# Four heads' queries and decays as a fifth set of half products, turned by transposes, and all heads' by way of memory

## The chip, the cores and the metric

One core of one Trainium2 chip runs the kernel. The metric is device time in microseconds for one execution, as the median of several runs.

## What is computed

A decoder trunk of two layers on 512 positions of width 2048, all in float32. Layer 0 runs a convolution branch and an attention branch; the change doesn't touch it. Layer 1 is a gated linear recurrence (HGRN2) with 16 heads, state 128x128:

```
h = rmsnorm(x, od_norm_g)
q, f_raw, i_val, g = split(h @ od_w_in)        # 2048 x 8192: four parts of 2048 columns
logf = logaddexp(log(lb), log1p(-lb) + log_sigmoid(f_raw));  k = -expm1(logf)
# per head, with b = cumsum(logf):
#   A[t,s] = sum_k q[t,k] k[s,k] exp(b[t]-b[s])  for s <= t
#   o      = A @ v + (q*exp(b)) @ state
o = rmsnorm(o, norm_g) * silu(g)
x = x + o @ od_w_out
```

After it comes a final rmsnorm. In the kernel `oq` names the query columns, `of` those of the decay, `oi` the values, `og` the gates. Each head has 128 columns of each.

## The kernel before

Every product is made in three matmuls of a high and a low part (`mm3`: high x high, low x high, high x low), so that the float32r matmuls of TensorE (PE) keep float32 precision. Weights come in tiles of 128x1024: the high part is read as it is, the low part is formed by ScalarE (ACT, the negated high part) and a second read that adds in memory (`Loaded`), or by a subtraction on VectorE (DVE) (`Formed`).

Layer 1 has three stages. First `dense("oq", h, h1)` and `dense("of", h, h1)` make queries and decays of heads 0 and 1, features on partitions, and write them to a DRAM tile `qd`. A `dense` is 4 quarters, each of 4 blocks x 3 matmuls of 512 columns, and after each quarter `tick()` runs.

Then values and gates are made by `SETS`, four sets of half products: seven products of half-size blocks in place of eight (Strassen's way, with sums of activation blocks in `sums` and of weight blocks in `Formed`). A product has 4 weight tiles, each with 2 blocks x 2 banks x 3 matmuls of 512 columns. Here positions are on partitions. `result` adds, scales by the row's reciprocal deviation `r1`, applies the gate's function where it is a gate, and writes to the DRAM tiles `vd` and `gd`.

Last the heads. While `dense` makes queries and decays of heads 2 to 15 straight into SBUF tiles `q` and `kn` (`m` for odd heads), `hgrn` runs as a generator: each `tick()` advances every live chain by one `yield`, so that the chain's own matmuls stand in PE's row after a quarter's 12. `begin_chain` starts the next head when its decay exists (`begun`) and enough ticks have passed since the last start (`since`: 8 for the first five and the last four, 10 for the others). A chain has 14 pieces: decays and their running products within 4 (`pi`, `xe`), two reciprocals, scaled queries and keys (`qb`, `kb` in `rc`), key products (L1073), two levels of `radix4` (L1026), transposes of keys (L1090), state updates (L1096), outputs (L1106, L1108), norm, and transposes of the result (L1125) into `mix[h]`. `out_part` puts parts of the output projection `w_out("ow", ...)` between the projections by the table `SPREAD`; `w_out` ticks once per column block.

PE's instructions run in the order in which the program writes them. On the other engines and on the DMA queues a planner orders them by its own estimates of when each is ready; each engine and queue then runs in that fixed order. SyncE (SP) issues the reads and writes of `qd`, `vd`, `gd`, `vr`, `gate` and of the residual `xall`; GpSimd (POOL) issues those of most weights. PSUM has 5 banks for `mm` and 3 for `aux`, which the chains use.

Of the kernel before, what the change touches and what calls it, by code (L numbers as in the profile page):

```python
# [7 lines left out]
F32 = mybir.dt.float32  # L8
# [7 lines left out]
P = 128  # L16
# [9 lines left out]
RATE = 0.67  # L26
RATE0 = 0.4
MAN = "PE"
N_WTILES = 224
N_EARLY = 128  # L30
LAST = 2 * N_WTILES - NK
SETS = [("oi", 0), ("oi", 1), ("og", 0), ("og", 1)]


V_EVG, V_ODG, V_FING = 0, 16, 32
# [14 lines left out]
def trunk(ctx: ExitStack, tc: tile.TileContext, x, w, ws, vec, cst, rope, msk, out, order):  # L50
# [28 lines left out]
    def spawn(gen):  # L79
        chains.append(gen)  # L80
        return gen
# [178 lines left out]
            act.activation(t, src, AF.Square)  # L260
            eng.tensor_tensor(out=acc, in0=acc, in1=t, op=ALU.add)

    def rstd_chain(acc, n, r, dst, delay=0, scale=None):


        accs = acc if isinstance(acc, tuple) else (acc,)
        nb = accs[0].shape[-1] // P
        for _ in range(delay):
            yield
        ps = ps_x()  # L270
        for b in range(nb):
            for i, a in enumerate(accs):
                pe.matmul(ps[:, b:b + 1], a[:, blocks(b)], ones[:, 0:1], start=i == 0, stop=i == len(accs) - 1)
        m = sm.tile([P, 4], F32, name="rm", tag="rm")
        dve.tensor_scalar(m[:, :nb], ps[:, 0:nb], 1.0 / n, EPS, op0=ALU.mult, op1=ALU.add)
        pool.tensor_tensor(out=r[:, :nb], in0=m[:, :nb], in1=nhalf[:, :nb], op=ALU.pow)
        if scale is not None:
            dve.tensor_scalar(r, r, scale, None, op0=ALU.mult)
        yield
        ps = ps_x()  # L280
        dg = tmp("c")
        for b in range(nb):
            dve.tensor_scalar(dg[:, blocks(b)], ident, r[:, b:b + 1], None, op0=ALU.mult)
        yield
        for b in range(nb):
            pe.matmul(ps[:, blocks(b)], ones, dg[:, blocks(b)], start=True, stop=True)
        if dst is not None:
            act.activation(dst, ps[:, :nb * P], AF.Copy)
        return ps
# [543 lines left out]
    xtx = ExitStack()  # L833
    xt = xtx.enter_context(tc.tile_pool(name="xt", bufs=1, reuse_waits="tile"))
    tpc[:] = [xt, "c"]
    c1 = spawn(rstd_chain(acc1, D, r1, rb1, 2))
    sums = [(fp.tile([P, 3 * H], F32R, name=f"fh{k}", tag=f"fh{k}"), fp.tile([P, 3 * H], F32R, name=f"fl{k}", tag=f"fl{k}"))
            for k in range(8)]

# [21 lines left out]
            split_scaled(u[:, j, :H], vs[:, V_ODG + k:V_ODG + k + 1], h1[k][0][:, H:], h1[k][1][:, H:])  # L861


    qd = [dr.tile([P, 2, S], F32, name=f"qd{h}") for h in range(2)]
    for h in range(2):
        ps = dense("oq", h, h1)
        if h == 0:
            for k in range(4):
                x_sums(k)
            finish(c1)  # L870
        z = tmp("z")
        dve.tensor_tensor(out=z, in0=ps, in1=rb1, op=ALU.mult)
        nc.sync.dma_start(qd[h][:, 0, :], z)
        ps = dense("of", h, h1)
        if h == 0:
            for k in range(4, 8):
                x_sums(k)
            xctx.close()
            xtx.close()
            ph.append(sctx.enter_context(tc.tile_pool(name="ph", bufs=1, reuse_waits="tile")))  # L880
        nc.sync.dma_start(qd[h][:, 1, :], decay(h, ps, tp.tile([P, S], F32, name="gate", tag="gate", bufs=2)))
# [47 lines left out]
    def keep(tag, b):  # L929
        return ph[0].tile([P, S], F32, name=tag, tag=f"{tag}{b}")  # L930

    for s_ in range(4):
        p1, p2 = banks(), banks()
        for m in range(4):
            product(p1, "A11", m)
# [26 lines left out]
            result(s_, 1, b, p3[b], u[b])  # L962
        for b in range(2):
            result(s_, 1, 2 + b, p7[b], u[b])
        if s_ == 3:
            restore()
        p4 = banks()
        for m in range(4):
# [10 lines left out]
    def hgt(name, shape=(P, S), tag=None):  # L979
        return hg.tile(list(shape), F32, name=name, tag=tag or name)  # L980

    at = hgt("at", (P, 4, P))
    pool.memset(at, 0.0)

    def blk(t_, half):
        return t_.rearrange("p (n c) -> p n c", c=8)[:, :, half * 4:half * 4 + 4]

    def to_at(ps, groups, cols, m, b0, nb, o):

        n = P // (4 * m)  # L990
        ng = len(groups)
        w = nb * m
        src = ps[:, :ng * 192].rearrange("p (g a n c) -> p g a n c", g=ng, a=2, n=n)[:, :, cols[0], :, cols[1] * m:
                                                                                     cols[1] * m + w]
        dst = at[:, groups[0]:groups[-1] + 1, :].rearrange("p g (n c) -> p g n c", c=4 * m)[:, :, :, b0 * m:b0 * m + w]
        msk_ = mk[:, None, o:o + n * w].broadcast_to([P, ng, n * w]).rearrange("p g (n c) -> p g n c", c=w)
        dve.copy_predicated(dst, msk_, src)

    def radix4(X, ks, t, m, ab, o):


        n = S // (4 * m)
# [19 lines left out]
        for gg in ((0, 1), (2, 3)):  # L1022
            ps = ps_x()
            for i, g in enumerate(gg):
                rhs = X[:, :, blocks(g)].rearrange("p a (n c) -> p a n c", c=4 * m)[:, :, :, m:]
                pe.matmul(ps[:, i * 192:(i + 1) * 192], ks[:, blocks(g)], rhs, start=True, stop=True)  # L1026
            to_at(ps, gg, (0, 0), m, 1, 3, o)
            to_at(ps, gg, (1, 0), m, 2, 2, o + 96)
            to_at(ps, gg, (1, 2), m, 3, 1, o + 160)
# [4 lines left out]
    vrows = {}  # L1034

    def hgrn(h, kn, q, gate):
        f = hgt("f")
        dve.tensor_scalar(f, kn, -(1.0 - 2.0 ** -24), 1.0, op0=ALU.max, op1=ALU.add)

# [89 lines left out]
    heads = []  # L1129
    qk = {}  # L1130

    def qk_tiles(h):
        qk[h] = (hg.tile([P, S], F32, name="q", tag="q", bufs=2), tmp("m", bufs=1) if h % 2 else hgt("kn"))
        return qk[h]

    def start(h):
        gate = tp.tile([P, S], F32, name="gate", tag="gate", bufs=2)
        nc.sync.dma_start(gate.rearrange("p (b c) -> p b c", b=4), gd[h // 4][:, :, blocks(h % 4)])
        q, kn = qk[h]
        heads.append(spawn(hgrn(h, kn, q, gate)))  # L1140

    for h in range(2):
        for i, t in enumerate(qk_tiles(h)):
            nc.sync.dma_start(t, qd[h][:, i, :])


    SPREAD = {0: [(6, 1, 3), (7, 0, 3), (7, 1, 3), (8, 0, 3), (8, 1, 2), (9, 0, 2)],
              1: [(9, 1, 3), (10, 0, 3), (10, 1, 3), (11, 0, 3), (11, 1, 2), (12, 0, 2)]}
    begun = [2]
    since = [99]  # L1150

    def begin_chain():
        since[0] += 1
        n = len(heads)
        if n < begun[0] and since[0] >= (8 if n < 5 else 10 if n < 12 else 8):
            since[0] = 0
            start(n)

# [9 lines left out]
                    w_out("ow", list(range(4 * g, 4 * g + 4)), range(c, c + part[2]))  # L1168
                c += part[2]

    for h in range(2, 16):
        if h == 4:
            spawn(load_xa(xd))
        ps = dense("oq", h, h1)
        q, kn = qk_tiles(h)
        dve.tensor_tensor(out=q, in0=ps, in1=rb1, op=ALU.mult)
        out_part(h, 0)
        decay(h, dense("of", h, h1), kn)
        begun[0] = h + 1
        out_part(h, 1)  # L1180
    w_out("ow", [8, 9, 10, 11], range(NK))
# [87 lines left out]
def _weights(inp, order):  # L1269
# [61 lines left out]
```

## Time and profile before

| | before |
|---|---|
| median of 3 runs | 1765.04 us (1764.37 to 1766.46) |
| profiled execution, its own time | 1763.39 us |
| span, first to last instruction | 1761.6 us |
| mean granted TensorE clock | 0.994 |
| PE busy | 1731.8 us (98%) |
| DVE busy | 1208.7 us (69%) |
| ACT busy | 735.5 us (42%) |
| POOL busy | 224.2 us (13%) |

The span is what the profile divides into engines' busy and idle time; the execution's own time is 1.8 us longer. Matmuls overlap in the records: one of 512 columns shows some 390 ns, and the next starts 227 ns after it, so PE's pace is read from the starts.

### The profile page before, as it was taken

Reading aid. Unit: us, or ns where it says so; the run is one execution under the profiler, and the core shown is the slowest. Engines: PE = TensorE matmul, PEld = TensorE weight load, DVE = VectorE, ACT = ScalarE, POOL = GpSimd, SP = SyncE. Lnnn points to the kernel's source line nnn. Section 1 sums busy time; section 2 is a strip of 40 time slices with the busy share of each in tenths; the row PEclk is TensorE's granted clock in tenths of the full one; section 3 lists DMA queues with packets and bytes.
Section 4 is the critical chain, followed back from the end, with each engine's and each line's share of the span. In section 5 each row is a group of like instructions: output and inputs, shape, how many; then the busy total and the mean of one; then the engine's idle time right before and its main releaser. Section 6 shows DMA issues by size and latency. Waiting matters only on the chain.

```text
span 1761.6 us, 22265 instructions
## 1 busy us (share of the span) xinstructions
PE 1731.8 (98%) x8227; PEld 1436.4 (82%) x8227; DVE 1208.7 (69%) x2268; ACT 735.5 (42%) x1345; POOL 224.2 (13%) x290
## 2 busy tenths in 40 slices
PE   8999999999999999999999999999999999999997
PEld 6888888888888888887788888888888888888896
DVE  8554948594889895575777678877567555557666
ACT  6434444444343233375545455533332333323354
POOL 6000000000000000051000000022222222222200
PEclk9999999999999999999999999999999999999998
DMA  6222222222373323268777676796677787887642
GB/s 236 94 89 86 83 99 82 96 84 90 98 237 101 99 93 102 96 193 240 234 234 218 230 221 218 219 285 153 146 180 162 159 193 161 169 190 158 150 132 96
DMA packets 93932, 273.34 MB, mean 155 GB/s; under 512 B 9344, under 2 KB 22912, under 8 KB 92928
## 3 DMA queue, kind: packets, MB, share of 16 engines
q1 hardware_dynamic: 66176, 172.38, 29.1%
q0 software_dynamic: 27072, 98.58, 26.4%
q8 instruction: 64, 1.05, 0.2%
q10 hardware_dynamic: 576, 0.97, 0.2%
q14 instruction: 44, 0.36, 0.1%
HBM read 250.93 MB, written 20.97 MB: 154 GB/s over the span
## 4 chain that ended last, share of the span: by engine, by line
PE 86%; DVE 7%; DMA 3%; issue 2%; ACT 2%; POOL 1%; POOLq 0%; DVEq 0%; ACTq 0%
PE mm L225 24%; PE mm L227 24%; PE mm L226 24%; PE aux L226 2%; PE aux L225 2%; PE aux L227 2%; PE aux L1026 2%; DMA rw<-ws 1%; PE aux L458 1%; PE aux L1106 1%; DVE hl L249 1%; DVE wl L253 1%; PE aux L1096 1%; PE aux L1073 1%; DVE wq L253 1%
## 5 line engine op out<-in xcount | busy, mean ns | idle before, releaser
L252 ACT ACTIVATE wq<-raw 128x512 fp32r<-128x512 f32 x256 | 161.0, 631 | 349.9 <-PE mm L227 342.7
L253 DVE TENSOR_TENSOR wq<-raw,wq 128x512 fp32r<-128x512 f32 x256 | 183.9, 720 | 120.2 <-ACT wq L252 119.5
L225 PE MATMUL mm<-hh,wq 128*128 128x512 f32 x656 | 263.0, 401 | 2.1 <-ACT wq L252 2.1
L227 PE MATMUL mm<-hh,wq 128*128 128x512 f32 x656 | 257.4, 392 | 2.7 <-DVE wq L253 2.7
L226 PE MATMUL mm<-hl,wq 128*128 128x512 f32 x656 | 256.9, 392 | 0.0
L225 PE MATMUL mm<-hh,wh 128*128 128x512 f32 x512 | 207.7, 406 | 0.0
L227 PE MATMUL mm<-hh,wl 128*128 128x512 f32 x512 | 200.2, 391 | 1.2 <-DMA wl<-w 1.2
L226 PE MATMUL mm<-hl,wh 128*128 128x512 f32 x512 | 199.6, 390 | 0.0
L170 ACT ACTIVATE wl<-wh 128x1024 fp32r<-128x1024 f32 x86 | 90.9, 1057 | 225.3 <-PE mm L227 214.6
L507 DVE SCALAR_TENSOR_TENSOR y<-u,cwh,y 128x512 f32<-128x512 f32 x240 | 178.8, 750 | 2.4
L227 PEld LDWEIGHTS mm<-hh,wq 128*128 128x128 f32 x656 | 123.9, 189 | 30.3 <-DVE wq L253 3.9
L225 PEld LDWEIGHTS mm<-hh,wq 128*128 128x128 f32 x656 | 124.1, 189 | 27.8 <-ACT wq L252 2.6
L226 PEld LDWEIGHTS mm<-hl,wq 128*128 128x128 f32 x656 | 124.1, 189 | 26.2 <-DVE hl L249 0.7
L227 PEld LDWEIGHTS mm<-hh,wl 128*128 128x128 f32 x512 | 96.1, 188 | 22.5 <-DMA wl<-w 1.6
L226 PEld LDWEIGHTS mm<-hl,wh 128*128 128x128 f32 x512 | 96.4, 188 | 17.7
L225 PEld LDWEIGHTS mm<-hh,wh 128*128 128x128 f32 x512 | 96.3, 188 | 17.4
L668 DVE TENSOR_TENSOR xall<-xall,mm 128x512 f32<-128x512 f32 x96 | 65.5, 683 | 62.9 <-PE mm L227 62.7
L252 ACT ACTIVATE wh<-rw 128x1024 fp32r<-128x1024 f32 x66 | 69.7, 1058 | 79.7 <-DMA rw<-ws 30.1
L225 PE MATMUL mm<-mh,wq 128*128 128x512 f32 x256 | 101.6, 397 | 0.0
L226 PE MATMUL mm<-ml,wq 128*128 128x512 f32 x256 | 101.3, 396 | 0.0
L227 PE MATMUL mm<-mh,wq 128*128 128x512 f32 x256 | 101.2, 395 | 0.0
L253 DVE TENSOR_TENSOR wl<-rw,wh 128x1024 fp32r<-128x1024 f32 x66 | 79.8, 1222 | 18.0 <-ACT wh L252 5.3
(312 smaller groups left out, 3592.6 us busy)
## 6 DMA issues: line engine op xcount, KB each, us to landing
raw<-w SPq DMA_DIRECT2D x127, 512.0 KB, 3.3
rw<-ws SPq DMA_DIRECT2D x96, 512.0 KB, 4.7
wh<-w POOLq DMA_DIRECT2D x86, 512.0 KB, 3.7
wl<-w POOLq DMA_DIRECT2D x86, 512.0 KB, 6.1
ts<-ws POOLq DMA_DIRECT2D x16, 512.0 KB, 5.4
xall<-xT SPq DMA_DIRECT2D x16, 256.0 KB, 4.9
xd<-xall SPq DMA_DIRECT2D x16, 256.0 KB, 2.5
vr<-vd SPq DMA_DIRECT2D x4, 1024.0 KB, 10.5
```

The lines of the kernel that those rows point to most:

```text
L170: act.activation(self.lo, self.hi.bitcast(F32), AF.Copy, scale=-1.0)
L225: pe.matmul(ps, a[0][:, asl], b[0][:, bsl], start=first, stop=False)
L226: pe.matmul(ps, a[0][:, asl], b[1][:, bsl], start=False, stop=False)
L227: pe.matmul(ps, a[1][:, asl], b[0][:, bsl], start=False, stop=last)
L249: dve.scalar_tensor_tensor(out=lo, in0=src, scalar=g, in1=hi.bitcast(F32), op0=ALU.mult, op1=ALU.subtract)
L252: act.activation(hi, src, AF.Copy)
L253: dve.tensor_tensor(out=lo, in0=src, in1=hi.bitcast(F32), op=ALU.subtract)
L458: pe.matmul(po[:, jb * P:], vr[:, jb, blocks(j)], pts[jb], start=jb == 0, stop=jb == 3)
L507: dve.scalar_tensor_tensor(out=y, in0=u[:, j:j + S], scalar=cwh[:, w0 + j:w0 + j + 1], in1=y, op0=ALU.mult, op1=ALU.add)
L668: dve.tensor_tensor(out=xa[c], in0=xa[c], in1=ps, op=ALU.add)
L1026: pe.matmul(ps[:, i * 192:(i + 1) * 192], ks[:, blocks(g)], rhs, start=True, stop=True)
L1073: pe.matmul(ps[:, blocks(g)], kb[:, blocks(g)], qb[:, blocks(g)], start=True, stop=True)
```

## The change

- A fifth set `("qf", 0)`: its first half of columns are the queries of heads 0 to 3, its second their decays. `result` writes the sums with positions on partitions to `qs`, for decays after the Tanh. Eight dense projections (16 weight tiles) go.
- `load_qk` reads a head's rows from `qs` for heads 0 to 3 and `turn_qk` turns them by 8 transposes on PE; ACT copies them out, and for the decay applies scale and bias there.
- Heads 4 and 5 (`ENTRY`) take the place of heads 0 and 1 before the sets. Heads 6 to 15 also go to DRAM (`qd`), and `load_qk` reads them back into `q` and `kn`.
- Queries are not scaled by the reciprocal deviation any more (ACT copies them); `er` puts its square into the epsilon of the head's norm instead.
- In a chain two reciprocals of 64 elements a partition and three multiplications replace two reciprocals of 256, in one piece less (13). X, the masked matrix `at` and the values `vr` have two buffers; `vr` is read head by head.
- A head starts every 7 ticks; `SPREAD` is written anew.

```diff
-N_WTILES = 224
+N_WTILES = 208
-SETS = [("oi", 0), ("oi", 1), ("og", 0), ("og", 1)]
+SETS = [("oi", 0), ("oi", 1), ("og", 0), ("og", 1), ("qf", 0)]
+ENTRY = (4, 5)
...
+        if er is not None:
+
+            dve.tensor_scalar(er, m, EPS, None, op0=ALU.mult)
...
-    for h in range(2):
+    for h in ENTRY:
...
-        dve.tensor_tensor(out=z, in0=ps, in1=rb1, op=ALU.mult)
+        act.activation(z, ps, AF.Copy)
...
+    qs = [dr.tile([P, 4, S], F32, name=f"qs{i}") for i in range(2)]
+
     def result(s_, col, b, in0, in1):
...
         dve.tensor_tensor(out=o, in0=in0, in1=in1, op=ALU.add)
+        if name == "qf":
+            if col:
+                act.activation(o, o, AF.Tanh, scale=rh[:, b:b + 1])
+            nc.sync.dma_start(qs[col][:, b, :], o)
+            return
...
-    at = hgt("at", (P, 4, P))
-    pool.memset(at, 0.0)
+    ats = [hgt("at", (P, 4, P)), cp.tile([P, 4, P], F32, name="at2", tag="acc")]
+    for at in ats:
+        pool.memset(at, 0.0)
...
+
         rc = hgt("rc")
-        dve.reciprocal(blk(rc, 0), blk(xe, 0))
-        yield
-        dve.reciprocal(blk(rc, 1), blk(pi, 1))
-        yield
+        r8, f8 = [a.rearrange("p (n c) -> p n c", c=8) for a in (rc, f)]
+        pool.memset(r8[:, :, 3], 1.0)
+        dve.reciprocal(r8[:, :, 0], xe.rearrange("p (n c) -> p n c", c=8)[:, :, 0])
+        dve.reciprocal(r8[:, :, 7], pi.rearrange("p (n c) -> p n c", c=8)[:, :, 7])
+        yield
+        dve.tensor_tensor(out=r8[:, :, 1:7:5], in0=r8[:, :, 0:8:7], in1=f8[:, :, 1:8:6], op=ALU.mult)
+        dve.tensor_tensor(out=r8[:, :, 2:6:3], in0=r8[:, :, 1:7:5], in1=f8[:, :, 2:7:4], op=ALU.mult)
+        dve.tensor_tensor(out=r8[:, :, 4], in0=r8[:, :, 5], in1=f8[:, :, 5], op=ALU.mult)
...
-        X, ks = hgt("X", (P, 2, S)), hgt("ks")
+        X, ks = hg.tile([P, 2, S], F32, name="X", tag="X", bufs=2), hgt("ks")
...
-        if h % 4 == 0:
-            vrows[h // 4] = hgt("vr", (P, 4, S))
-            nc.sync.dma_start(vrows[h // 4], vd[h // 4])
...
-        dve.tensor_scalar(rs, ss, 1.0 / P, EPS, op0=ALU.mult, op1=ALU.add)
+
+        dve.scalar_tensor_tensor(out=rs, in0=ss, scalar=1.0 / P, in1=er, op0=ALU.mult, op1=ALU.add)
...
-    def qk_tiles(h):
-        qk[h] = (hg.tile([P, S], F32, name="q", tag="q", bufs=2), tmp("m", bufs=1) if h % 2 else hgt("kn"))
-        return qk[h]
+    def load_qk(h):
+        qk[h] = (hg.tile([P, S], F32, name="q", tag="q", bufs=2), hgt("kn"))
+        if h > 3:
+            for i, t in enumerate(qk[h]):
+                nc.sync.dma_start(t, qd[h][:, i, :])
+            return
+        rows.extend((tmp("z"), tmp("m", bufs=1)))
+        for i, t in enumerate(rows):
+            nc.sync.dma_start(t.rearrange("p (b c) -> p b c", b=4), qs[i][:, :, blocks(h)])
+
+    rows = []
+
+    def turn_qk(h):
+
+        for i, t in enumerate(rows):
+            pt = ps_x()
+            for b in range(4):
+                pe.transpose(pt[:, blocks(b)], t[:, blocks(b)], ident)
+            if i == 0:
+                act.activation(qk[h][0], pt, AF.Copy)
+            else:
+                act.activation(qk[h][1], pt, AF.Identity, scale=la[:, h:h + 1], bias=nla[:, h:h + 1])
+        rows.clear()
 
     def start(h):
         gate = tp.tile([P, S], F32, name="gate", tag="gate", bufs=2)
         nc.sync.dma_start(gate.rearrange("p (b c) -> p b c", b=4), gd[h // 4][:, :, blocks(h % 4)])
+        vr = hg.tile([P, 4, P], F32, name="vr", tag="vr", bufs=2)
+        nc.sync.dma_start(vr, vd[h // 4][:, :, blocks(h % 4)])
...
+    SPREAD = {0: [(11, 0, 8), (11, 1, 8)],
+              1: [(12, 0, 4), (12, 1, 4), (13, 0, 8)]}
+    begun = [6]
+    since = [2]
 
     def begin_chain():
         since[0] += 1
         n = len(heads)
-        if n < begun[0] and since[0] >= (8 if n < 5 else 10 if n < 12 else 8):
+        if n not in qk and n < begun[0] and since[0] >= (2 if n < 4 else 4):
+            load_qk(n)
+        if rows and since[0] >= 6:
+            turn_qk(n)
+        if n in qk and since[0] >= 7:
             since[0] = 0
             start(n)
...
-    for h in range(2, 16):
-        if h == 4:
+    for h in range(6, 16):
+        if h == 8:
             spawn(load_xa(xd))
+        qd[h] = dr.tile([P, 2, S], F32, name=f"qd{h}")
         ps = dense("oq", h, h1)
-        q, kn = qk_tiles(h)
-        dve.tensor_tensor(out=q, in0=ps, in1=rb1, op=ALU.mult)
+        z = tmp("z")
+        act.activation(z, ps, AF.Copy)
+        nc.sync.dma_start(qd[h][:, 0, :], z)
         out_part(h, 0)
-        decay(h, dense("of", h, h1), kn)
+        nc.sync.dma_start(qd[h][:, 1, :], decay(h, dense("of", h, h1), tmp("m", bufs=1)))
         begun[0] = h + 1
```

## Rows read from the trace of the kernel before

**Rows 1.** The page's busy time, share of the span and instructions of each engine.

```profile
PE 1731.8 (98%) x8227; PEld 1436.4 (82%) x8227; DVE 1208.7 (69%) x2268; ACT 735.5 (42%) x1345; POOL 224.2 (13%) x290
```

**Rows 2.** Windows: length; busy us (instructions) of PE, PEld, DVE, ACT, POOL; clock, DMA, GB/s.

```profile
900.00:976.00 76.00, 76.00 (x337) 62.90 (x336) 55.45 (x54) 39.52 (x42) 3.45 (x4) 1.00 0.73 217
...
1150.00:1200.00 50.00, 50.00 (x250) 42.58 (x249) 36.53 (x100) 16.64 (x38) 12.84 (x19) 1.00 1.01 273
...
1189.75:1219.55 29.80, 28.68 (x148) 24.34 (x147) 19.29 (x54) 10.50 (x27) 7.41 (x12) 1.00 0.69 151
...
1620.00:1680.00 60.00, 60.00 (x307) 51.05 (x306) 42.72 (x114) 19.00 (x51) 14.27 (x21) 1.00 0.71 153
```

**Rows 3.** Waits of PE, whole span: us in total, times, longest.

```profile
PE aux L1026 <- DVE X L1012: 4.5, 4, 1.1
...
PE aux L1125 <- DVE on L1121: 0.7, 1, 0.7
```

**Rows 4.** Timeline of PE, half products and heads: start, duration, instruction, idle before it.

```profile
1101.60 0.39 PE L225 MATMUL mm<-wh,fh 128*128 128x512 f32 x1
...
1104.09 0.39 PE L227 MATMUL mm<-wh,fl 128*128 128x512 f32 x1
...
1193.38 0.60 PE L1125 MATMUL aux<-cs,on 128*128 128x128 f32 x4
1193.81 1.47 PE L1026 MATMUL aux<-X,ks 128*128 128x192 f32 x8
...
1201.86 1.54 PE L1026 MATMUL aux<-X,ks 128*128 128x192 f32 x8 [1.12 <-DVE X L1012]
```

**Rows 5.** Groups by form, from 1100 us on: busy, mean ns, idle before.

```profile
L1054 DVE RECIPROCAL rc<-xe 128x256 f32<-128x256 f32 x16 | 28.0, 1749 | 0.0
L1056 DVE RECIPROCAL rc<-pi 128x256 f32<-128x256 f32 x16 | 27.9, 1742 | 0.0
...
L1048 DVE TENSOR_TENSOR pi<-pi,f 128x128 f32<-128x128 f32 x48 | 19.0, 395 | 6.4 <-ACT pi L1045 6.2
```

**Rows 6.** Timeline of DVE ahead of the wait at 1201.86.

```profile
1199.83 1.75 DVE L1056 RECIPROCAL rc<-pi 128x256 f32<-128x256 f32 x1
1201.49 0.23 DVE L1012 TENSOR_TENSOR X<-X,ab 128x128 f32<-128x128 f32 x1
```

**Rows 7.** DMA issues, 1150 to 1170 us: count, KB each, median us to landing.

```profile
gd<-z SPq DMA_DIRECT2D x1, 256.0 KB, 4.5
gd<-gate SPq DMA_DIRECT2D x1, 256.0 KB, 12.3
gate<-gd SPq DMA_DIRECT2D x1, 256.0 KB, 7.2
```

**Rows 8.** DMA issues, 1120 to 1720 us.

```profile
gate<-gd SPq DMA_DIRECT2D x16, 256.0 KB, 3.1
xall<-xd SPq DMA_DIRECT2D x16, 256.0 KB, 12.8
...
gd<-z SPq DMA_DIRECT2D x3, 256.0 KB, 3.0
...
kn<-qd SPq DMA_DIRECT2D x1, 256.0 KB, 5.3
```

**Rows 9.** Timeline of PE after the decay matmuls of head 15.

```profile
1644.35 1.46 PE L1026 MATMUL aux<-X,ks 128*128 128x192 f32 x8
1645.51 0.53 PE L225 MATMUL mm<-mh,wh 128*128 128x512 f32 x1
...
1662.17 1.05 PE L1073 MATMUL aux<-qb,rc 128*128 128x128 f32 x8
```

**Rows 10.** Timeline of DVE in the same stretch, first and last step to the scaled keys.

```profile
1647.53 0.42 DVE L1038 TENSOR_SCALAR f<-m 128x512 f32<-128x512 f32 x1
...
1656.46 0.45 DVE L1063 TENSOR_TENSOR rc<-m,rc 128x256 f32<-128x256 f32 x1
```

**Rows 11.** Timeline of ACT in the same stretch, the decay.

```profile
1646.16 0.82 ACT L769 ACTIVATE m<-th,nla,la 128x512 f32<-128x512 f32 x1
```

More of the change, by code (lines that the diff above doesn't have):

```diff
@@ L261, in add_square, with rstd_chain @@
             eng.tensor_tensor(out=acc, in0=acc, in1=t, op=ALU.add)
-    def rstd_chain(acc, n, r, dst, delay=0, scale=None):
+    def rstd_chain(acc, n, r, dst, delay=0, scale=None, er=None):
         accs = acc if isinstance(acc, tuple) else (acc,)
@@ L835, in trunk @@
     tpc[:] = [xt, "c"]
-    c1 = spawn(rstd_chain(acc1, D, r1, rb1, 2))
+    er = cp.tile([P, 4], F32, name="er")
+    c1 = spawn(rstd_chain(acc1, D, r1, rb1, 2, er=er))
     sums = [(fp.tile([P, 3 * H], F32R, name=f"fh{k}", tag=f"fh{k}"), fp.tile([P, 3 * H], F32R, name=f"fl{k}", tag=f"fl{k}"))
@@ L861, in x_diff @@
             split_scaled(u[:, j, :H], vs[:, V_ODG + k:V_ODG + k + 1], h1[k][0][:, H:], h1[k][1][:, H:])
-    qd = [dr.tile([P, 2, S], F32, name=f"qd{h}") for h in range(2)]
-    for h in range(2):
+    qd = {h: dr.tile([P, 2, S], F32, name=f"qd{h}") for h in ENTRY}
+    for h in ENTRY:
         ps = dense("oq", h, h1)
-        if h == 0:
+        if h == ENTRY[0]:
             for k in range(4):
@@ L871, in trunk @@
         z = tmp("z")
-        dve.tensor_tensor(out=z, in0=ps, in1=rb1, op=ALU.mult)
+        act.activation(z, ps, AF.Copy)
         nc.sync.dma_start(qd[h][:, 0, :], z)
         ps = dense("of", h, h1)
-        if h == 0:
+        if h == ENTRY[0]:
             for k in range(4, 8):
@@ L930, in keep @@
         return ph[0].tile([P, S], F32, name=tag, tag=f"{tag}{b}")
-    for s_ in range(4):
+    for s_ in range(len(SETS)):
         p1, p2 = banks(), banks()
@@ L964, in trunk @@
             result(s_, 1, 2 + b, p7[b], u[b])
-        if s_ == 3:
+        if s_ == len(SETS) - 1:
             restore()
@@ L980, in hgt, with to_at @@
         return hg.tile(list(shape), F32, name=name, tag=tag or name)
-    at = hgt("at", (P, 4, P))
-    pool.memset(at, 0.0)
+    ats = [hgt("at", (P, 4, P)), cp.tile([P, 4, P], F32, name="at2", tag="acc")]
+    for at in ats:
+        pool.memset(at, 0.0)
     def blk(t_, half):
         return t_.rearrange("p (n c) -> p n c", c=8)[:, :, half * 4:half * 4 + 4]
-    def to_at(ps, groups, cols, m, b0, nb, o):
+    def to_at(at, ps, groups, cols, m, b0, nb, o):
         n = P // (4 * m)
@@ L997, in to_at, with radix4 @@
         dve.copy_predicated(dst, msk_, src)
-    def radix4(X, ks, t, m, ab, o):
+    def radix4(at, X, ks, t, m, ab, o):
         n = S // (4 * m)
@@ L1026, in radix4 @@
                 pe.matmul(ps[:, i * 192:(i + 1) * 192], ks[:, blocks(g)], rhs, start=True, stop=True)
-            to_at(ps, gg, (0, 0), m, 1, 3, o)
-            to_at(ps, gg, (1, 0), m, 2, 2, o + 96)
-            to_at(ps, gg, (1, 2), m, 3, 1, o + 160)
+            to_at(at, ps, gg, (0, 0), m, 1, 3, o)
+            to_at(at, ps, gg, (1, 0), m, 2, 2, o + 96)
+            to_at(at, ps, gg, (1, 2), m, 3, 1, o + 160)
         dve.tensor_tensor(out=x0[:, :, 1:4, :], in0=x0[:, :, 1:4, :], in1=bc(ab[:, :, 0:3], 3), op=ALU.mult)
@@ L1032, in radix4, with hgrn @@
         dve.tensor_tensor(out=k4[:, :, 0:3, :], in0=k4[:, :, 0:3, :], in1=bc(ab[:, :, 4:7], 3), op=ALU.mult)
-    vrows = {}
-    def hgrn(h, kn, q, gate):
+    def hgrn(h, kn, q, gate, vr):
+        at = ats[h % 2]
         f = hgt("f")
@@ L1076, in hgrn @@
         ab = hgt("ab", (P, 16, 8))
-        yield from radix4(X, ks, t8, 8, ab, P)
+        yield from radix4(at, X, ks, t8, 8, ab, P)
         yield
-        if h % 4 == 0:
-            vrows[h // 4] = hgt("vr", (P, 4, S))
-            nc.sync.dma_start(vrows[h // 4], vd[h // 4])
         t32 = ab.rearrange("p (n b) c -> p n b c", b=4)[:, :, :, 3]
         ab2 = hgt("ab2", (P, 4, 8))
-        yield from radix4(X, ks, t32, 32, ab2, P + 192)
+        yield from radix4(at, X, ks, t32, 32, ab2, P + 192)
         yield
         yield
-        vr = vrows[h // 4][:, :, blocks(h % 4)]
         pt = ps_x()
@@ L1138, in start @@
         nc.sync.dma_start(gate.rearrange("p (b c) -> p b c", b=4), gd[h // 4][:, :, blocks(h % 4)])
+        vr = hg.tile([P, 4, P], F32, name="vr", tag="vr", bufs=2)
+        nc.sync.dma_start(vr, vd[h // 4][:, :, blocks(h % 4)])
         q, kn = qk[h]
[L1140 to L1150, printed above, removed]
+        heads.append(spawn(hgrn(h, kn, q, gate, vr)))
+    SPREAD = {0: [(11, 0, 8), (11, 1, 8)],
+              1: [(12, 0, 4), (12, 1, 4), (13, 0, 8)]}
+    begun = [6]
+    since = [2]
     def begin_chain():
@@ L1298, in _weights @@
     for n, (name, a) in enumerate(SETS):
-        c0 = {"oi": 4096, "og": 6144}[name] + a * 1024
-        b = od[:, c0:c0 + 1024].reshape(2, 4, 2, P, 2, S)
+        c0 = [S * a, 2048 + S * a] if name == "qf" else [{"oi": 4096, "og": 6144}[name] + a * 1024 + i * S for i in range(2)]
+        b = np.concatenate([od[:, c:c + S] for c in c0], 1).reshape(2, 4, 2, P, 2, S)
         ws[n] = b.transpose(0, 4, 1, 3, 2, 5)
```

## The prediction

> **What bounds the kernel now.** I read the page first: TensorE (PE) is busy 98% of the span, DVE 69% [rows 1]. Then the stages: in the half products PE has no idle time, in the stage of the heads little, and the clock is granted in full in both; DVE is two thirds busy [rows 2]. The PE's waits say what idle time is left there: 4.5 us in four waits for one DVE multiply, 0.7 us in another [rows 3]. So the time is the sum of PE's instructions plus a few stalls, and an edit is worth what it takes out of PE's row, less what it makes PE wait. Of PE's order all is written by hand; a chain of a head gets one piece after each quarter (12 matmuls of 512 columns), so a late piece stops PE.
>
> **Matmuls removed and added.** A projection is 4 quarters, 48 matmuls of 512 columns. Eight go (queries and decays of heads 0 to 3): 384. A set of half products is 7 products x 4 x 2 x 2 x 3 = 336. Saved: 48. In the half products 11 matmuls take 1104.09 - 1101.60 = 2.49 us, 0.2264 each [rows 4]; a stretch of 76 us holds 337 [rows 2], which agrees, and a dense quarter has the same step. 48 x 0.2264 = **-10.9 us**. What the fifth set needs beside PE (splits on ACT and DVE, 28 half-megabyte reads) the other sets hide wholly: in a set ACT works 39.5 of 76 us, DVE 55.5, PE never idles [rows 2]. If that cover went, PE would wait there by the set.
>
> **Transposes added.** Eight groups of four 128-column transposes. Such a group ran from 1193.38 to 1193.81, 0.43 us, before the next instruction [rows 4]: 8 x 0.43 = **+3.4 us**. Below it can't be, since they stand on PE; above, if each cost its whole duration, about 0.27 us (0.60 less three steps of 0.11), it is 32 x 0.27 = 8.6. I take the step, since matmuls too show durations above their steps. The Trainium skill ("TensorE: Matmul & The Clock Gate", "Part 4: PE-mode transpose") gives about 275 ns for a transpose within a kernel and says that transposes don't count as busy for the clock in the same way; by that figure these 32 would cost 8.8 us and eat most of the saving, which makes it a rival below. The trace disagrees so far: a step of 0.11 us, and a granted clock of 1.00, the 2.4 GHz level, in the stage that has such groups [rows 2, 4].
>
> **The chain of a head.** Two reciprocals of 256 elements, 1.75 and 1.74 us [rows 5], become two of 64 and three multiplies. By elements 64 cost about 0.5; a 128-element multiply is 0.395 [rows 5], with steps near 0.3, so the five take about 1.8 us: 1.7 saved on DVE a head. One of the old reciprocals is what PE waits for: in order on DVE stand a multiply into X, the reciprocal of the next head (1199.83), and the second multiply (1201.49), and PE's L1026 starts at 1201.86 after 1.12 us of idle [rows 4, 6]. Without 1.75 us in between the wait is gone. The four such waits and the 0.7: **-5.2 us** (bounds 0, if other work takes the place, and -5.2).
>
> Heads start every 7 quarters instead of 8 or 10. A head now takes 29.8 us with 8 quarters and 1.1 of stall, so its own PE work is 29.8 - 1.1 - 8 x 2.72 = 6.9; 7 quarters give 25.9 us. DVE has 19.3 us in that head [rows 2], less 1.7 and less 0.7 for the query's multiply, which goes to ACT: 16.9 of 25.9, 65% as before. So no engine becomes the bound, and closer starts alone make PE no shorter, as they add and remove no matmul. The POOL memset, the doubled X and masks, the small reads of values and the rescaled epsilon stand beside other work; query and decay traffic adds some 15 MB (56 transfers of 256 KB), on DMA engines that are 0.7 busy in that stage [rows 2]. The stretch with 1.01 shows no PE idle [rows 2], so weights stay ahead. For new small collisions (three auxiliary banks are shared with the turning) I put **+1 us** (0 to 5).
>
> **The first head.** Its query rows need the last two results of the fifth set. After the end E of the set: additions and issue 1.5 us, store 4.5, load 7.2, both from the stretch where the reads of the residual (xall) crowd in [rows 7]: E + 13.2. PE turns these rows after 4 quarters, E + 10.9. **+2 us** (0 with the short times of rows 8, 1.5 + 3.0 + 3.1 = 7.6; 8 if the load sits in the crowd for 12.8). Behind that load on SP's queue wait the residual's reads, wanted some 40 quarters later.
>
> **The last heads.** I counted quarters from the thresholds. The stage falls from 160 to 128 quarters; head n starts at 5 + 7n, until the supply ends it: the decay of heads 13, 14 and 15 is ready at quarters 96, 104 and 112, and the chain starts one quarter later, as now. But now query and decay take the way through memory and are read back in that same quarter, where heads up to 12 are read at least three quarters ahead. After the last decay matmul the trace has (head 15): PE goes on to the next instruction at 1644.35, the decay is written by 1646.98, so 2.6 us [rows 9, 10, 11]; then store 3.0 and load 3.1 [rows 8], round trip 6.1; then from f (1647.53) to the last scaled key (1656.91) 9.4 now [rows 10], 7.7 with the short reciprocals, 5.3 without the additions and state updates in between; I take 6.4. Together 15.2 us. PE asks for it after 4 quarters and three auxiliary steps of the head before: 1662.17 - 1645.51 is five quarters and these steps [rows 9], 16.7, less one quarter 13.9, and 13.7 at the dense pace. It waits 1.5 us, three times: **+4.5 us**. Bounds: 0; and a store of 4.5 with a load of 5.3 [rows 7, 8] make the round trip 9.8 and the wait 5.2, 15.6 in all. Behind the late instruction on DVE stand the state updates of the head before and, for head 15, additions to the residual; five PSUM banks cover those. The Trainium skill ("DMA: Bandwidth & Descriptors", "Anatomy of one DMA - SWDGE (gpsimd) path") has about 2 us fixed in any DMA, whatever its size; two in a row then can't go under 4, and the rows say 6.1.
>
> **Sum.** -10.9 + 3.4 - 5.2 + 1 + 2 + 4.5 = -5.2 us on the profiled execution's 1763.39: 1758.2. The median of the runs is 1.65 above that execution: **1759.8 us**.
>
> **Rivals.** A change under 0.2% (3.5 us) can't be told from none.
> *Slower, by the round trip.* Where the three last heads meet crowded queues, 9.8 us for store and load, the sum is -5.2 - 4.5 + 15.6 = +5.9, 1770.9. Without this term the sum is -9.7: a wait of 3.2 a head (round trip 7.8) makes a tie, 4.4 (9.0) a loss that shows. For it: the decay's rows of now that came back from memory took 5.3, and more traffic shares the queues. Against it: sixteen gate loads in just that stage have a median of 3.1 [rows 8]. Chance 0.17.
> *The DVE waits stay.* Heads lie closer, and other pieces of the next head slip between the two multiplies: 4 x 1.1 + 0.7 stay, the sum is 0.0, 1765.0. For it: the same two quarters between the two L1026 groups. Against: nothing as long as 1.75 us is left on DVE, and late in the stage, where heads also follow at 8 quarters, PE has no idle time (60.00 of 60 us) [rows 2]. 0.22.
> *The first head sits in the crowd*: 8 for 2 us, +0.8, 1765.8; for it a store of 12.3 behind three residual reads [rows 7]; against it that here the stores go out before them. 0.07.
> *Transposes cost their duration*: 8.6 for 3.4, 0.0, 1765.0. 0.03.
> *All the waits are hidden*: SP gets the row in time and the last heads fit, -10.9 + 3.4 - 5.2 = -12.7, 1752.3. For it: the wait of 1.5 is a small difference of large times. 0.13.
>
> **Numbers.** The forecast itself has 0.38, with 1756 to 1761.5. Faster: 0.38 + 0.13 = 0.51; same: 0.22 + 0.07 + 0.03 = 0.32; slower 0.17. The range takes in the hidden case but its edge, and most of the round trip's: 1753 to 1770.
>
> **What would show it.** Right: five sets with no PE idle in the fifth; transposes of a group at steps of 0.11; no wait of L1026 for X; a few us at the first turning; waits of 1 to 3 us at the key products (L1073 of now) of heads 13, 14 and 15, with the decay's load just ahead; heads 25.9 us apart. Wrong: PE waits at every head (the closer spacing doesn't fit DVE), waits for weights in the stage of the heads, or a round trip far from 6 us.

## The result, and the profile after

| | before | after |
|---|---|---|
| median | 1764.70 us (4 runs, 1763.49 to 1766.46) | 1790.86 us (4 runs, 1790.32 to 1792.63) |
| span of the profiled execution | 1761.6 us | 1789.4 us |
| mean granted TensorE clock | 0.994 | 0.986 |

The ratio is 1.0144, 95% interval 1.0130 to 1.0159: the changed kernel is 26 us slower. It was forecast at 1759.8.

The page's busy time of the changed kernel shows a PE as busy as before [rows 1] in a span that is 27.8 us longer:

```profile
PE 1731.7 (97%) x8211; PEld 1436.6 (80%) x8211; DVE 1225.6 (68%) x2351; ACT 760.4 (42%) x1379; POOL 210.1 (12%) x279
```

So the loss is idle time of PE, and its waits name it. These are all that the stage of the heads has (1200 to 1700 us); L1090 are the key products (L1073 before), L1163 the new turning transposes. The waits for X [rows 3] are gone.

```profile
PE aux L1090 <- DVE rc L1080: 25.3, 3, 8.8
PE aux L1163 <- DMA z<-qs: 6.4, 1, 6.4
```

The three are heads 13, 14 and 15. Windows show where there is no loss and then the way into the first of these waits (columns as in [rows 2]): the fifth set of half products, the heads with 7 quarters between starts, and after them store, read and idle stretch of head 13.

```profile
1148.50:1224.50 76.00, 76.00 (x337) 62.89 (x336) 57.58 (x62) 39.80 (x47) 5.08 (x8) 1.00 0.72 215
1300.00:1570.00 270.00, 270.00 (x1421) 231.98 (x1421) 194.84 (x615) 100.51 (x279) 72.61 (x117) 1.00 0.83 193
1585.60:1591.10 5.50, 5.50 (x30) 4.68 (x29) 0.70 (x2) 1.72 (x3) 1.36 (x2) 1.00 0.98 214
1591.15:1598.40 7.25, 5.47 (x32) 4.41 (x30) 0.02 (x1) 0.00 (x0) 0.00 (x1) 1.00 0.81 190
1598.40:1604.60 6.20, 0.00 (x0) 0.00 (x0) 5.51 (x17) 1.77 (x10) 0.68 (x1) 0.67 0.00 1
```

The timelines of ACT, of SP's queue and of DVE give each link of head 13, as [rows 9 to 11] did for head 15. ACT ends the decay at 1585.54:

```profile
1584.73 0.81 ACT L773 ACTIVATE m<-th,nla,la 128x512 f32<-128x512 f32 x1
```

SP issues its store at once, and the read back when the store has landed, 5.6 us later:

```profile
1585.57 0.33 SPq L1217 DMA_DIRECT2D qd<-m  x1
1591.15 0.33 SPq L1150 DMA_DIRECT2D kn<-qd  x1
```

DVE gets the decay at 1598.38, 7.2 us after that, and has the scaled keys at 1604.51:

```profile
1583.12 0.69 DVE L770 TENSOR_TENSOR z<-mm,rb 128x512 f32<-128x512 f32 x1 [0.97 <-PE mm L228]
...
1598.38 0.43 DVE L1050 TENSOR_SCALAR f<-kn 128x512 f32<-128x512 f32 x1 [7.46 <-DMA kn<-qd]
...
1604.09 0.42 DVE L1080 TENSOR_TENSOR rc<-kn,rc 128x256 f32<-128x256 f32 x1
```

The DMA issues of 1560 to 1690 us (columns as in [rows 7]) say the same of all three heads; in [rows 8] store and read took 3.0 and 3.1.

```profile
qd<-m SPq DMA_DIRECT2D x3, 256.0 KB, 5.4
kn<-qd SPq DMA_DIRECT2D x3, 256.0 KB, 7.9
```

And PE's timeline shows a second price behind the wait:

```profile
1596.23 0.39 PE L228 MATMUL mm<-hh,wl 128*128 128x512 f32 x1
1604.65 2.04 PE L1090 MATMUL aux<-qb,rc 128*128 128x128 f32 x8 [8.03 <-DVE rc L1080]
1606.34 0.77 PE L226 MATMUL mm<-hh,wh 128*128 128x512 f32 x1
...
1607.34 0.63 PE L228 MATMUL mm<-hh,wl 128*128 128x512 f32 x1
1607.77 0.63 PE L226 MATMUL mm<-hh,wh 128*128 128x512 f32 x1
...
1610.74 0.39 PE L227 MATMUL mm<-hl,wh 128*128 128x512 f32 x1
1610.97 0.40 PE L228 MATMUL mm<-hh,wl 128*128 128x512 f32 x1
```

After 8.03 us without work the matmuls start 0.43 us apart, nearly twice 0.227: the 1.2 GHz level. Ten take 1610.74 - 1606.34 = 4.40 us in place of 2.26, and the eight key products 1606.34 - 1604.65 = 1.69 in place of 0.81 (the same eight of head 0, 1255.43 to 1256.24). That is 3.0 us more for the head. Behind the waits of heads 14 and 15 the low level ends sooner:

```profile
1644.71 2.04 PE L1090 MATMUL aux<-qb,rc 128*128 128x128 f32 x8 [8.53 <-DVE rc L1080]
1646.40 0.77 PE L226 MATMUL mm<-hh,wh 128*128 128x512 f32 x1
...
1648.26 0.40 PE L227 MATMUL mm<-hl,wh 128*128 128x512 f32 x1
...
1684.01 2.04 PE L1090 MATMUL aux<-qb,rc 128*128 128x128 f32 x8 [8.78 <-DVE rc L1080]
1685.71 0.77 PE L226 MATMUL mm<-mh,wh 128*128 128x512 f32 x1
...
1689.25 0.39 PE L228 MATMUL mm<-mh,wl 128*128 128x512 f32 x1
```

The key products lose 0.9 us each time; four matmuls take 1.86 us in place of 0.91, and eight take 3.54 in place of 1.82. So the three heads lose 3.0, 1.8 and 2.6 us this way, 7.4 in all.

### The profile page after: what moved, and what is told of

Its sections match the earlier page's. It is cut to its first block, busy times and chain, and to the rows that moved or that the text cites. A ratio compares the mean times of both kernels' runs of the same rounds, so it can differ in the third digit from the quotient of the medians.

```text
span 1789.4 us, 22560 instructions
## 1 busy us (share of the span) xinstructions
PE 1731.7 (97%) x8211; PEld 1436.6 (80%) x8211; DVE 1225.6 (68%) x2351; ACT 760.4 (42%) x1379; POOL 210.1 (12%) x279
## 4 chain that ended last, share of the span: by engine, by line
PE 84%; DMA 6%; DVE 5%; issue 3%; ACT 2%; POOL 0%; POOLq 0%; DVEq 0%; ACTq 0%; SPq 0%
PE mm L226 23%; PE mm L228 23%; PE mm L227 23%; PE aux L227 2%; PE aux L226 2%; PE aux L228 2%; PE aux L1039 2%; DMA kn<-qd 1%; PE aux L1090 1%; DMA rw<-ws 1%; PE aux L462 1%; DMA qd<-m 1%; DVE wl L254 1%; DVE hl L250 1%; PE aux L1119 1%
## 5 line engine op out<-in xcount | busy, mean ns | idle before, releaser
L226 PE MATMUL mm<-hh,wh 128*128 128x512 f32 x384 | 158.4, 412 | 0.0
L228 PE MATMUL mm<-hh,wl 128*128 128x512 f32 x384 | 151.5, 395 | 0.2 <-DMA wl<-w 0.2
L227 PE MATMUL mm<-hl,wh 128*128 128x512 f32 x384 | 151.0, 393 | 0.0
L253 ACT ACTIVATE wh<-rw 128x1024 fp32r<-128x1024 f32 x82 | 86.6, 1058 | 95.6 <-DMA rw<-ws 35.6
L171 ACT ACTIVATE wl<-wh 128x1024 fp32r<-128x1024 f32 x70 | 74.2, 1060 | 121.2 <-PE mm L228 107.1
L254 DVE TENSOR_TENSOR wl<-rw,wh 128x1024 fp32r<-128x1024 f32 x82 | 99.1, 1221 | 20.9 <-PE aux L227 5.7
L254 DVE TENSOR_TENSOR wl<-ts,wh 128x1024 fp32r<-128x1024 f32 x60 | 72.2, 1221 | 31.4 <-ACT wh L253 19.6
L228 PEld LDWEIGHTS mm<-hh,wl 128*128 128x128 f32 x384 | 72.8, 190 | 16.6 <-DMA wl<-w 0.6
L227 PEld LDWEIGHTS mm<-hl,wh 128*128 128x128 f32 x384 | 73.5, 191 | 13.5
```

What stands on the lines that cost most here:

```text
L171: act.activation(self.lo, self.hi.bitcast(F32), AF.Copy, scale=-1.0)
L226: pe.matmul(ps, a[0][:, asl], b[0][:, bsl], start=first, stop=False)
L227: pe.matmul(ps, a[0][:, asl], b[1][:, bsl], start=False, stop=False)
L228: pe.matmul(ps, a[1][:, asl], b[0][:, bsl], start=False, stop=last)
L253: act.activation(hi, src, AF.Copy)
L254: dve.tensor_tensor(out=lo, in0=src, in1=hi.bitcast(F32), op=ALU.subtract)
```

## The experiments

Theory: the three last heads lose some 11 us each, because their decay is stored and read back within the quarter in which it is wanted, beside the weights' reads. Rivals: closer starts on DVE, the added transposes, the first turning, or a total that belongs to no single head. Unless a diff says otherwise, a kernel is the changed one with one edit; ratios are against the kernel before.

**The last three heads without memory.** Query and decay of heads 13 to 15 go straight into their tiles (`e1_direct`); with two heads only, head 13 stays by memory (`e8_dose`: `h >= 14`).

```diff
+        if h >= 13:
+            q = hg.tile([P, S], F32, name="q", tag="q", bufs=2)
+            act.activation(q, ps, AF.Copy)
+            out_part(h, 0)
+            ps = dense("of", h, h1)
+            kn = hgt("kn")
+            decay(h, ps, kn)
+            qk[h] = (q, kn)
```

> The changed kernel with queries and decays of heads 13, 14 and 15 written straight into the tiles that the chain reads, not by way of memory; all else as changed. Theory (late read-back): the three waits of PE for the scaled keys, 25.3 us, and what the clock at 1.2 GHz costs after each, some 3 us each, go: 1790.9 - 25.3 - 9 = about 1756.6 us, with the 6.4 us at the first turning left. Rival (heads every 7 quarters are too close for DVE and the queues): the waits of these heads come back at other places and the time stays above 1775 us.

> Heads 14 and 15 direct, head 13 by memory as changed: one late head of three. If each late head costs by itself (8 us of wait and 3 of the low clock): 1756.8 + 11 = about 1768 us. Rival (the loss comes from the three in a row, each late by the one before): clearly under 1763 us.

`e1_direct`: 1756.78 us, 0.9954 (0.9942 to 0.9967). `e8_dose`: 1770.33, 1.0028 (1.0017 to 1.0039). All three waits go, and one comes back with head 13. The waits of `e8_dose`:

```profile
PE aux L1090 <- DVE rc L1080: 8.5, 1, 8.5
PE aux L1163 <- DMA z<-qs: 6.4, 1, 6.4
```

One head costs 0.0074 of the time, 13 us; three cost 0.0190, 33.5 us, 11.2 each. The loss belongs to each head by itself, and without it the change is a gain.

**Lighter weights.** The last 20 weight tiles ahead of the final stage get no second read, and their low part is zero: these products lack the term of the weights' low part.

```diff
-            act.activation(self.lo, self.hi.bitcast(F32), AF.Copy, scale=-1.0)
-            pool.dma_start(self.lo, self.src, accum_op=ALU.add)
+            act.activation(self.lo, self.hi.bitcast(F32), AF.Copy, scale=0.0 if self.light else -1.0)
+            if not self.light:
+                pool.dma_start(self.lo, self.src, accum_op=ALU.add)
...
-            items.append(Loaded(w[i]) if 2 * i < LAST else Kept(w[i], 2 * i - LAST))
+            items.append(Loaded(w[i], i >= 180) if 2 * i < LAST else Kept(w[i], 2 * i - LAST))
```

> The changed kernel, but for the last 20 weight tiles before the final stage the second read, which forms the low part, is left out (the low part is zero there, so these products lack their low-part term); it takes away half of the weights' traffic around heads 13 to 15. If the way through memory is slow because the weights' reads fill the DMA engines: the round trip falls from 13 us to about 6, the waits from 8.4 to about 1.5 each, the clock stays up after them, 1762 to 1768 us. Rival (the round trip is a fixed cost of a write and a read that depends on it): the waits stay at 8 us and the time at 1788 to 1791 us.

1761.08 us, 0.9986 (0.9976 to 0.9995). The DMA issues of 1560 to 1700 us and the waits of this kernel (L1093 are the key products):

```profile
qd<-m SPq DMA_DIRECT2D x3, 256.0 KB, 2.0
kn<-qd SPq DMA_DIRECT2D x3, 256.0 KB, 2.5
```

```profile
PE aux L1093 <- DVE rc L1083: 2.0, 3, 0.9
```

The same store and read take 4.5 us in place of 13.3, and three waits of 25.3 us in all shrink to 2.0; both are better than was expected. In 1560 to 1640 us the DMA share is 0.38 here and 0.68 in the changed kernel. So the round trip's length is the traffic beside it, not the way through memory as such. What went away are the reads that add in memory, half of the weights' bytes; whether as many plain reads would lengthen it as much was not run.

**Start later.** A head starts three quarters after its read was issued.

```diff
-        if n in qk and since[0] >= 7:
+        if n in qk and since[0] >= 7 and loaded[n] >= 3:
```

> The changed kernel, where every head starts at least 3 quarters after its read from memory is issued; that moves the start of heads 13, 14 and 15 alone, by 3 quarters each. Late read-back: 3 quarters are 8.2 us and some auxiliary work, about the wait of 8.4, so the waits fall to 0 to 1 us each; the last chain ends with the last quarter, so 1 to 3 us may come at the end: 1757 to 1763 us. Rival (the queue or DVE cannot follow at all): waits of more than 5 us each stay and the time stays above 1775 us.

1780.64 us, 1.0085 (1.0065 to 1.0105): most of the loss stays. The key products no longer wait, but older heads do. PE's waits and DVE's timeline:

```profile
PE aux L1139 <- DVE on L1135: 9.1, 1, 9.1
...
PE aux L1103 <- DVE ks L1045: 4.1, 2, 3.9
```

```profile
1602.90 0.43 DVE L1050 TENSOR_SCALAR f<-kn 128x512 f32<-128x512 f32 x1 [8.49 <-DMA kn<-qd]
...
1611.08 0.69 DVE L1135 TENSOR_TENSOR on<-on,gate 128x512 f32<-128x512 f32 x1 [0.66 <-ACT on L1134]
```

DVE's order is fixed ahead. The late head's first instruction, f, still stands early in it, waits 8.49 us for the read, and behind it wait the norm and gate of an older head, for which PE now stops. To tell that, the next kernel also puts f (on DVE) and the first copy of a head's chain (on ACT) behind all work written before them, for heads 13 to 15 (`e10_behind`).

```diff
+        with ordered(h, dve):
+            dve.tensor_scalar(f, kn, -(1.0 - 2.0 ** -24), 1.0, op0=ALU.max, op1=ALU.add)
...
+        with ordered(h, act):
+            act.activation(pi4[:, :, 0], f4[:, :, 0], AF.Copy)
```

> The kernel whose late heads start 3 quarters after their read (1780.6 us), and for heads 13 to 15 the first DVE and ACT steps of the chain are queued behind all that the program wrote ahead of them on these engines. Theory (the late read stops DVE's and ACT's fixed rows, in which the first step of the new head stood ahead of older heads' work): the waits for older heads, 9.1 us for a result and 4.1 us for keys, go; PE waits less than 3 us in all for these heads, 1757 to 1765 us. Rival (the time is lost by the traffic of the way itself, wherever the steps stand): 1775 to 1781 us.

1765.30 us, 1.0010 (0.9999 to 1.0021), with store and read still 5.0 and 7.7 us. All waits from 1570 to 1720 us are now:

```profile
PE aux L1116 <- ACT kst L1112: 2.0, 1, 2.0
PE mm L227 <- DVE ml L250: 1.8, 1, 1.8
PE aux L1146 <- DVE on L1142: 0.5, 1, 0.5
PE aux L1097 <- DVE rc L1087: 0.5, 1, 0.5
```

Between the two kernels 0.0075 of the time, 13 us (about 4 either way), is the place of these instructions in the queues. The waits listed are 4.8 us, more than the 3 expected, and the time lies 0.3 us above the expected range. It is also still 0.0056, some 10 us (about 3 either way), above `e1_direct`; what of that is not these waits stays open.

**The first turning.** Two quarters later for head 0's rows (`e4_turn`), and the same with the direct last heads (`e7_both`).

```diff
-    since = [2]
+    since = [0]
```

> The changed kernel with all heads 2 quarters later (the first turning after 6 quarters instead of 4; heads 13 to 15 are bound by the supply and start as changed, but for head 13, one quarter later). Theory (the query rows of head 0 land late behind the residual's reads): the wait of 6.4 us falls by 2 quarters, 5.4 us, to about 1, and some of the low clock after it goes; head 13 waits 2.7 us less: 1779 to 1785 us. Rival (the read waits for the queue's crowd, and moves with it): the wait stays at 6 us, 1788 to 1791 us.

> The two mendings together: heads 13 to 15 direct, and all heads 2 quarters later so that the first turning comes after 6 quarters. If the two losses are apart: 1756.8 less the wait of 6.4 and 1 to 2 us of the low clock after it, 1748 to 1750 us, 0.8% under the kernel before. Rival (the read of head 0's rows moves with the crowd, or another wait takes the place): 1754 to 1757 us.

1780.04 us, 1.0095 (1.0081 to 1.0108), and 1759.19, 0.9974 (0.9961 to 0.9987): `e7_both` is no better than `e1_direct`. PE's waits of `e7_both` and its DVE's timeline show that the wait only moved:

```profile
PE aux L1090 <- DVE rc L1080: 5.7, 1, 5.7
...
PE aux L1163 <- DMA z<-qs: 0.8, 1, 0.8
```

```profile
1256.47 0.69 DVE L770 TENSOR_TENSOR z<-mm,rb 128x512 f32<-128x512 f32 x1 [8.73 <-issue]
1257.08 0.41 DVE L1079 TENSOR_TENSOR rc<-kn,xe 128x256 f32<-128x256 f32 x1
```

In DVE's fixed order the first multiply of the next decay, which writes a tile z, stands ahead of head 0's scaled keys, and DVE did nothing for 8.73 us before it. It was not waiting for PE's sums: PE's last matmul before its own wait started at 1251.84, 4.6 us earlier. The multiply started as the store of head 6's queries, which also leaves from a tile z, landed: SP issued that store at 1241.00, six residual reads (xall) from 1241.63 on, and the store took 15.4 us, to 1256.4. The DMA issues of 1236 to 1262 us:

```profile
qd<-z SPq DMA_DIRECT2D x1, 256.0 KB, 15.4
```

So here too a late transfer stops DVE's row, and a chain behind it. `e4_turn` shows the same 15.4 us and a wait of 5.8; its time lies in the expected range for another reason: the last heads lost less, 9.6 us in two waits for keys and 4.0 in two at L1121. Why they did stays open.

**What makes that read late.** In the changed kernel SP issues head 0's row read at 1230.83 and seven residual reads (xall) from 1232.40 on; the rows land at 1241.9, after 11 us. With the direct last heads, the residual's reads are queued behind head 0's row reads (`e9_order`) or behind head 1's too (`e11_apart`, `reads[:4]`).

```diff
+                for r in behind or ():
+                    es.enter_context(tc.issue_after(r))
+                nc.sync.dma_start(xa[k], src[:, k, :])
...
-            spawn(load_xa(xd))
+            spawn(load_xa(xd, reads[:2]))
```

> Heads 13 to 15 direct (1756.8 us), and on SP's queue the residual's reads stand behind the two reads of head 0's rows. Theory (at the first turning PE waits 6.4 us because that read sits in the crowd of the residual's reads): store and read then meet the weights alone, about 8 to 10 us after the set where PE asks at 10.9, so the wait falls to 0 to 1 us, the low clock after it goes as well: 1748 to 1750 us. Rival (the weights' reads alone make it late, or the next read is late in its place): a wait of 4 us or more is left, 1754 to 1757 us.

> Heads 13 to 15 direct, and the residual's reads stand on SP's queue behind the reads of head 1's rows too, which wait until PE has turned head 0's rows: so nothing of the residual moves while head 0's rows are read. Theory (the residual's reads, even those issued behind, slow that read): it lands in 3 to 6 us in place of 11.2, PE's wait at the first turning falls from 6.3 to 0 to 2 us, the low clock after it goes: 1748 to 1752 us, 0.8% under the kernel before. Rival (the weights' reads alone slow it, as at heads 13 to 15): 7 us or more for the read, a wait of 2 to 6 us, 1753 to 1757 us.

`e9_order`: 1757.64 us, 0.9956 (0.9941 to 0.9972), no gain: the residual's reads go out right behind and the row read still takes 11.2 us. `e11_apart`: 1753.09 us, 0.9946 (0.9934 to 0.9958), the lowest median, but by the ratios not told apart from `e1_direct`. The outcome lies between theory and rival: the read took 6.7 us (3 to 6, or 7 and more), the wait of 1.8 us is the theory's, and the time, 1 us above the theory's range, is the rival's. SP's queue in `e9_order`, then in `e11_apart`:

```profile
1230.55 0.53 SPq L1157 DMA_DIRECT2D z<-qs  x1
...
1232.16 10.57 SPq L652 DMA_DIRECT2D xall<-xd  x8
```

```profile
1231.72 0.53 SPq L1157 DMA_DIRECT2D z<-qs  x1
...
1241.10 4.38 SPq L652 DMA_DIRECT2D xall<-xd  x7
```

PE's timeline has the transposes after 6.33 us of idle in the one and 1.78 in the other:

```profile
1241.74 1.12 PE L1167 MATMUL aux<-cs,z 128*128 128x128 f32 x4 [6.33 <-DMA z<-qs]
```

```profile
1238.39 0.66 PE L1167 MATMUL aux<-cs,z 128*128 128x128 f32 x4 [1.78 <-DMA z<-qs]
```

So transfers issued after a read made it longer, 11.2 against 6.7 us (11.0 in `e1_direct`, 6.3 in `e12_apart1`). The DMA share during the read was 1.02 in both, so the share alone does not give the price of a transfer. With the start one quarter later as well (`since = [1]`, `e12_apart1`):

> As the run with the residual's reads kept apart, and all heads one quarter (2.7 us) later. If a wait of up to 2 us is left at the first turning there, it goes here and the time is 1747 to 1750 us; if the weights alone slow the read, 2.7 us less wait than there; if the wait moves to the keys of head 0, as with two quarters, no gain.

1754.97 us, 0.9950 (0.9938 to 0.9962): the last 1.8 us of wait go, two of 1.2 and 0.9 come, no gain that can be told.

**The short reciprocals alone**, in the kernel before.

```diff
-        dve.reciprocal(blk(rc, 0), blk(xe, 0))
+        dve.reciprocal(r8[:, :, 0], xe.rearrange("p (n c) -> p n c", c=8)[:, :, 0])
+        dve.reciprocal(r8[:, :, 7], pi.rearrange("p (n c) -> p n c", c=8)[:, :, 7])
...
+        dve.tensor_tensor(out=r8[:, :, 1:7:5], in0=r8[:, :, 0:8:7], in1=f8[:, :, 1:8:6], op=ALU.mult)
```

> The kernel before with one part of the change alone: the short reciprocals and three multiplications in place of the long reciprocals, in the same number of pieces. Theory (the four waits of 1.1 us come from the long reciprocal between two multiplies into X): they go, 1763.8 - 4.5 = about 1759.3 us. Rival (any work of the next head makes that wait): 1763 to 1764 us, four waits left.

1759.68 us, 0.9968 (0.9956 to 0.9980), 5.1 us (2.1 either way) less than the 1764.77 of the kernel before. Of [rows 3] 0.7 us in four waits is left:

```profile
PE aux L1026 <- DVE X L1012: 0.7, 4, 0.2
```

**The price of a transpose.** `e1_direct` with every turning transpose made four times, 96 more.

```diff
-            for b in range(4):
+            for b in list(range(4)) * 4:
```

> The kernel with the last three heads direct (1756.8 us), in which each turning makes its transposes four times over: 128 in place of 32. Theory (a transpose costs its step, 0.11 us): 96 x 0.11 = 10.6 more, about 1767 us. Rival (it costs its recorded duration of about 0.27 us): 26 more, about 1783 us; or the clock falls in them, more still.

1768.60 us, 1.0023 (1.0012 to 1.0034). Against `e1_direct` that is 0.0069, 12.2 us, or 0.127 us a transpose, about 3 us either way in the sum by the two intervals; at 0.27 each it would be 26. PE's timeline has both clock levels, head 0's turning after 6.58 us of idle, then head 1's:

```profile
1247.55 3.68 PE L1163 MATMUL aux<-cs,z 128*128 128x128 f32 x16 [6.58 <-DMA z<-qs]
1251.01 3.17 PE L1163 MATMUL aux<-cs,m 128*128 128x128 f32 x16
1253.93 0.47 PE L226 MATMUL mm<-hh,wh 128*128 128x512 f32 x1
...
1275.31 1.91 PE L1163 MATMUL aux<-cs,z 128*128 128x128 f32 x16
1277.05 1.91 PE L1163 MATMUL aux<-cs,m 128*128 128x128 f32 x16
```

At the full clock sixteen take 1.74 us, 0.109 each; after the idle 3.46 us, 0.216 each.

## Why the prediction was wrong

The right mechanism stood among the rivals ("slower, by the round trip") with a chance of 0.17, and its price was too small: +5.9 us there, 26 measured.

| Term | forecast, us | measured, us |
|---|---|---|
| 48 matmuls less | -10.9 | not separated; fits below |
| 32 transposes | +3.4 | +3.5 to 4.1 (0.109 to 0.127 each) |
| waits for X | -5.2 | -5.1 (2.1 either way) alone; gone in the changed kernel |
| small collisions | +1 | none seen |
| first head | +2 | 6.4 of wait, 1.7 of low clock |
| last three heads | +4.5 | 25.3 of waits, 7.4 of low clock |
| sum | -5.2 | 28.1 by these terms; span +27.8 |

The measured sum, with -10.9, 3.4 and -5.2 as forecast, lies 0.3 us above the growth of the span; both sides are one execution each. `e11_apart`, with the last heads direct and 1.8 us of wait, comes to -10.9 + 3.4 - 5.2 + 1.8 = -10.9, and its median is 10.8 below that of the kernel before (the interval allows 2.1 either way).

**The step that failed** is "store 3.0 and load 3.1 [rows 8], round trip 6.1" in the last heads' term. The other links held for head 13: from the decay's sums on PE (1583.1) to the decay written 2.4 us (2.6 forecast), from f to the last scaled key 6.1 (6.4), PE's work until it asks, to 1596.6, 13.5 (13.7 to 13.9). Only the round trip was 12.8 in place of 6.1, and 6.7 more turn a wait of 1.5 into 8.0. (The forecast's 2.6, 6.1 and 6.4 add up to 15.1, not 15.2, which changes nothing.) The durations came from gate reads and stores at other moments; here store and read lie among the weights' reads, with DMA shares of 0.98 and 0.81 in just those stretches, and `e3_light` shows 4.5 us once the adding half of those weights' traffic is gone. Mean share of the stage, 0.7 [rows 2], said nothing about that, and the upper bound of 9.8 was added up from two single transfers (4.5 and 5.3), so it was too low as well.

The Trainium skill ("DMA: Bandwidth & Descriptors", "Anatomy of one DMA - SWDGE (gpsimd) path") puts about 2 us fixed into a DMA on GpSimd's path. SyncE issues the transfers here; their 2.0 and 2.5 in `e3_light` lie near it, and the 5.4 and 7.9 of the changed kernel show how much the traffic beside them adds.

**A term was missing**: the clock after a wait. 1.8 to 3.0 us a late head and 1.7 at the first turning, 9.1 us in all, stood in no sum.

**The first head** took the mechanism named (rows read among the residual's reads), with a read of 11 us for 7.2. That the stores go out ahead of the residual's reads, my argument against the crowd, did not help: the read itself has them behind it.

**What held**: no idle of PE in the fifth set (76.00 of 76.00 us); transposes by step, not duration; short reciprocals of 0.54 and 0.49 us that take PE's waits away, so the rival in which they stay falls; heads 25.7 us apart (key products of three in a row at 1335.19, 1360.92 and 1386.64 us; 25.9 forecast), with no wait at this spacing in 270 us, so DVE is not the bound, though it was busy 194.84 of 270 us, 72% where 65% was forecast.

The Trainium skill ("TensorE: Matmul & The Clock Gate", "Part 4: PE-mode transpose") gives some 275 ns for a transpose, measured in bf16; by that the 96 of `e6_four`, in float32, would cost an estimated 26 us, and they cost 12.2. Its other sentence, that transposes don't count as busy for the clock in the same way, is not contradicted: see below.

## What to carry to other kernels

A tile that is stored and read back costs nothing only as long as something else lies between; where the consumer is due in the same few microseconds, price store and read by rows from a stretch with the same transfers around them, not by medians over a stage or the DMA share. Delaying the consumer does not help while its first instruction keeps its early place in an in-order queue: move that place, or skip the memory. And price a wait of PE with what the matmuls after it lose at the lower clock.

## What the runs showed of the hardware

- A 256 KB store and the read of it took 5.4 and 7.9 us beside the weights' reads, 2.0 and 2.5 with the half of these that adds in memory gone.
- Reads issued later on the same queue made an earlier read longer: 11.2 us with the residual's reads behind it, 6.7 with them held back 9 us. A store with six of these reads behind it took 15.4.
- Waits of 8.0, 8.5 and 8.8 us were followed by 6.1, 3.6 and 5.2 us at the 1.2 GHz level, which cost 3.0, 1.8 and 2.6 us more. In `e6_four`, after 6.58 us of idle, 32 transposes took 6.38 us (at the full clock's step 3.5), most of it at that level, while in the changed kernel eight transposes (1.62 us) and five matmuls (2.13 us) saw the clock back. One stretch of each does not settle whether transposes hold it down; at the full clock the same 32 in a row kept it.
